# A hybrid diffusion step in fp32: input modulation split differently over the engines, and a spread-out residual chain

## Chip, cores and metric

One core of one Trainium2 chip. The metric is the device time of one execution in microseconds (us); the profile is one execution on the same core, with the time of every instruction.

## What is computed

The reference is one inference step of a two-layer backbone on 640 tokens (128 context tokens and 512 latent ones) of width 2048, in fp32. Cut to what matters here:

```python
for l in range(DEPTH):
    hp = rmsnorm(xp, norm_pre[l]) * (1.0 + sc_p[:, None]) + sh_p[:, None]
    hs = rmsnorm(xs, norm_pre[l]) * (1.0 + sc_s[:, None]) + sh_s[:, None]
    ...
    xp = xp + g_p[:, None] * rmsnorm(op, norm_post[l])
    xs = xs + g_s[:, None] * rmsnorm(os_, norm_post[l])
```

Between the two stands the layer's mixer: an input projection of h, attention (layer 0) or retention (layer 1), a gate, and an output projection to op and os_. Shift sh and scale sc are vectors over the 2048 features, one for the context and one for the latent tokens; they come from a small product of the conditioning with w_ada.

## The kernel before

Everything lies transposed: features on the 128 partitions in 16 tiles (KT = 16), the 640 tokens along the free dimension. Tokens come in two groups, columns 0 to 384 (GROUPS[0], 128 context and 256 latent tokens) and 384 to 640 (GROUPS[1]). An fp32 product is made of three faster ones: each operand is split into a rounded high half and the remainder (hi and lo for activations, whi and wlo for weights), and hi x whi, lo x whi and hi x wlo are summed in PSUM. A split takes a copy with rounding on ScalarE (ACT) and a subtraction on VectorE (DVE).

**Slots.** The four big projections are one list of slots. A slot has one piece of weight of 128 x 512: its load on the SP queue, its split (split_slot, lines 277 and 278, four slots ahead: there are four buffers for whi and wlo), and its products on TensorE (PE, line 1374; line 1315 for a layout that is transposed). A 128-column block of output takes four slots. In an output projection the 16 blocks of group 0 come first and then those of group 1, 64 slots each.

**Lanes.** All other work is queued by hand in lanes (class Lane). An item of a lane is a list of stages. One call of step() runs one stage of each item in flight, oldest first, and then takes up to `new` further items whose needs are done, and runs their first stage. step_all() is called once per slot ahead of the slot's products; the split of the slot four ahead is issued behind them. Thus the program order of every engine is fixed by the lanes, and an instruction that waits holds all that is behind it on its engine.

**The start (lines 286 to 479).** For 64 steps u, a piece of w_ada (512 KB of "ada" rows, on the SP queue, eight buffers) is multiplied with the conditioning on TensorE (a_mm, line 328). Four steps give one row of shift and scale for one tile kt: row() adds four partial rows on VectorE (lines 370 and 372), turn() transposes them on TensorE (line 376), mods() forms sh and am on VectorE. The input x lies in y. Before the loop its squares are summed and the norm factor is spread over all partitions (rbc). The lanes of the start run in the order d_l, s_l, x_l, w_l, h_l. In s_l, scale_x multiplies a tile of x by rbc on POOL (GpSimd). In x_l, mod_x applies am and sh on VectorE (two instructions, since context and latent tokens have different columns), and split_x makes hi on ScalarE and lo on VectorE. w_l splits the first weights (lines 415 and 416). d_l multiplies (first_dense, line 425): each step's products stand on TensorE between the a_mm of two steps.

**The residual chain (queue_chain, from line 911).** When the last block of a group's output projection is evacuated, its chain is queued. For layer 0 it holds: the norm (n1 with sums on TensorE, n2, rbc); for each tile n a residual item res(n), with r1 multiplying y by rbc (on VectorE for even n, on POOL for odd n), r2 adding x on VectorE, r3 squaring on ScalarE, r4 adding to the sum acc2 on POOL, and a store to x1; then a second norm; then for each tile an item hk(n): h1 multiplies by rbc on VectorE, h2 applies am and sh on POOL, h3 makes hi on ScalarE, h4 makes lo on VectorE. The last h4 sets ("h1", group). The chain of group 0 so runs beside the 64 slots of group 1's output projection, with one item begun per slot (new = 1); the chain of group 1 runs beside the first 32 slots of the next projection w_in_odd, which are for group 0 alone, with two per slot (new = 2). Before w_in_odd uses a group, all steps that are left up to ("h1", group) are run at once. Beside the chain evac_out squares every finished block on ScalarE and adds it on POOL (line 886), once in four slots.

Of the kernel before, what the change touches and what calls it, by code (L numbers as in the profile page):

```python
# [11 lines left out]
F32 = mybir.dt.float32  # L12
F32R = mybir.dt.float32r
BF16 = mybir.dt.bfloat16
AF = mybir.ActivationFunctionType
ALU = mybir.AluOpType
# [6 lines left out]
T = TP + TS  # L23
# [139 lines left out]
def body(tc, io):  # L163
    nc = tc.nc
# [6 lines left out]
    hi = main.tile([128, KT, T], F32R, name="hi")  # L171
    lo = main.tile([128, KT, T], F32R, name="lo")
    y = main.tile([128, KT, T], F32, name="y")
# [8 lines left out]
    sh = [main.tile([128, KT, 2], F32, name=f"sh{l}") for l in range(2)]  # L182
    am = [main.tile([128, KT, 2], F32, name=f"am{l}") for l in range(2)]
# [47 lines left out]
    def parts(c0, c1):  # L231

        return [(a, b, v) for a, b, v in ((c0, min(c1, TP), 0), (max(c0, TP), c1, 1)) if a < b]

    def unperm(dst, m0, nm):

        return dst.rearrange("p (r m c) -> p m r c", r=8, m=4)[:, m0:m0 + nm]
# [18 lines left out]
    for job, (w, kind, role, col, gs) in enumerate(STREAM):  # L256
        u0 = FIRST_UNIT[BLOCK_AT[w, kind, col]]
        n = UNITS[kind]
# [23 lines left out]
    with ExitStack() as st:  # L282
        s1 = st.enter_context(tc.tile_pool(name="s1", bufs=1))
        sraw = st.enter_context(tc.tile_pool(name="sraw", bufs=SRAW))
        x = y
# [47 lines left out]
        done = set()  # L333
        h_l, d_l = Lane(done), Lane(done)
# [14 lines left out]
        rbc = s1.tile([128, T], F32, name="rbc0")  # L349
# [15 lines left out]
        def queue_h(kt):  # L365
            t = {}

            def row():
                t["row"] = r = s1.tile([2, 256], F32, name="adarow", bufs=2)
                nc.vector.tensor_copy(r, rowps[kt][0:2, :256])  # L370
                for j in range(1, 4):
                    nc.vector.tensor_tensor(r, r, rowps[kt][32 * j:32 * j + 2, :256], op=ALU.add)

            def turn():
                for i in range(2):
                    nc.tensor.transpose(rowps[kt][:, 256 + 2 * i:258 + 2 * i], t["row"][:, 128 * i:128 * i + 128],
                                        ident[:2, :2])

            def mods():
                ps = rowps.pop(kt)  # L380
                nc.vector.tensor_scalar(sh[0][:, kt, :], ps[:, 256:258], cols[:, 0, 2, kt:kt + 1], None, op0=ALU.add)
                nc.vector.tensor_scalar(am[0][:, kt, :], ps[:, 258:260], bsc1[:, kt:kt + 1], cols[:, 0, 0, kt:kt + 1],
                                        op0=ALU.add, op1=ALU.mult)
                done.add(("mods", kt))

            def scale_x():
                nc.gpsimd.tensor_tensor(x[:, kt, :], x[:, kt, :], rbc, op=ALU.mult)
                done.add(("scaled", kt))

            def mod_x():  # L390
                u = x[:, kt, :]
                for a, b, v in parts(0, T):
                    nc.vector.tensor_scalar(u[:, a:b], u[:, a:b], am[0][:, kt, v:v + 1], sh[0][:, kt, v:v + 1],
                                            op0=ALU.mult, op1=ALU.add)

            def split_x():
                u = x[:, kt, :]
                nc.scalar.activation(hi[:, kt, :], u, AF.Copy)
                nc.vector.tensor_tensor(lo[:, kt, :], u, hi[:, kt, :].bitcast(F32), op=ALU.subtract)
                done.add(("h", kt))  # L400

            h_l.add([row, None, turn, mods], [("row", kt)])
            s_l.add([scale_x], ["rbc"] + ([("mods", kt - 1)] if kt > 1 else []))
            x_l.add([mod_x, split_x], [("mods", kt), ("scaled", kt)])

        def queue_d(q):
            ns, kt, after = FIRST_SEQ[q]
# [30 lines left out]
            w_l.add([split_w], ["rbc", ("w", q), ("row", min(after, KT - 1))] + ([("d", q - 3)] if q > 2 else []))  # L438
            d_l.add([None] + [first_dense(n) for n in range(4)], [("h", kt), ("wsplit", q)])

        x_l, s_l, w_l = Lane(done), Lane(done), Lane(done)
        for kt in range(KT):
            queue_h(kt)
        for q in range(len(FIRST_SEQ)):
            queue_d(q)
        lanes0 = (d_l, s_l, x_l, w_l, h_l)

        def squares(i):
            for kt in range(4 * i, 4 * i + 4):
# [39 lines left out]
    done = set()  # L489
    heads = Lane(done)  # L490
    rope = Lane(done)
    chain = Lane(done)
# [418 lines left out]
    def queue_chain(l, gi):  # L911
# [50 lines left out]
        def res(n):  # L962
            v = y[:, n, a:b]
            t = {}

            def r1():
                (nc.gpsimd if n % 2 else nc.vector).tensor_tensor(v, v, st["rbc"][:, :w], op=ALU.mult)  # L967

            def r2():
                nc.vector.tensor_tensor(v, v, c["x", 8 * gi + n // 2][:, n % 2, :w], op=ALU.add)  # L970

            def store():
                if n % 2:
                    nc.sync.dma_start(dst[:, n - 1:n + 1, a:b], y[:, n - 1:n + 1, a:b])
                    i = 8 * gi + n // 2
                    if i < 3:
                        free("kkq"[i])
                    else:
                        load_x(l, i + 3)

            def r3():
                t["sq"] = cp.tile([128, 384], F32, name="sq2", bufs=2)
                nc.scalar.activation(t["sq"][:, :w], v, AF.Square)

            def r4():
                if n == 0:
                    c["acc2", gi] = cp.tile([128, w], F32, name=f"acc2{gi}")
                    nc.vector.tensor_copy(c["acc2", gi], t["sq"][:, :w])
                elif n == KT - 1:
                    c["acc2", gi] = [c["acc2", gi], t["sq"]]  # L990
                    done.add(("acc2", l, gi))
                else:
                    nc.gpsimd.tensor_tensor(c["acc2", gi], c["acc2", gi], t["sq"][:, :w], op=ALU.add)

            return [r1, r2, r3, r4, store]

        def hk(n):
            t = {}

            def h1():  # L1000
                t["u"] = cp.tile([128, 384], F32, name="u", bufs=6)
                nc.vector.tensor_tensor(
                    t["u"][:, :w], y[:, n, a:b], st["rbc"][:, :w], op=ALU.mult)

            def h2():
                u = t["u"]
                for a2, b2, v in parts(a, b):
                    nc.gpsimd.tensor_scalar(u[:, a2 - a:b2 - a], u[:, a2 - a:b2 - a], am[1][:, n, v:v + 1],  # L1008
                                            sh[1][:, n, v:v + 1], op0=ALU.mult, op1=ALU.add)

            def h3():
                nc.scalar.activation(hi[:, n, a:b], t["u"][:, :w], AF.Copy)

            def h4():
                nc.vector.tensor_tensor(lo[:, n, a:b], t["u"][:, :w], hi[:, n, a:b].bitcast(F32), op=ALU.subtract)
                if n == KT - 1:
                    done.add(("h1", gi))

            return [h1, h2, h3, h4]

        chain.add([None, n1("acc"), None, n2, flag("rbc")])
        for n in range(0, KT, 2 if last else 1):
            chain.add((res_pair if last else res)(n), [("rbc", l, gi)] if n == 0 else ())
            if last and gi == 0:
                chain.add([None])
        if not last:
            chain.add([None, None, None, n1("acc2"), None, n2, flag("rbc2")], [("acc2", l, gi)])
            for n in range(KT):
                chain.add(hk(n), [("rbc2", l, gi)] if n == 0 else ())


    R = {}
# [484 lines left out]
```

## Time and profile before

| what | value |
| --- | --- |
| median of 3 runs | 2555.88 us (2555.37 to 2557.2) |
| the profiled execution | 2555.74 us |
| its span in the profile | 2553.9 us |
| TensorE busy | 2466.1 us (97%) |
| VectorE busy | 1507.5 us (59%) |
| ScalarE busy | 994.0 us (39%) |
| POOL busy | 485.3 us (19%) |
| moved by DMA | 347.12 MB, 136 GB/s on average |

The span runs from the first to the last instruction. A busy TensorE is not TensorE at its peak: products are pipelined, their ends are modelled, and two may overlap in the table. So the pace of a stage is read from the distance of the starts of something that returns in every fourth slot, and not from the busy share. An arrow with a name behind a time says what the engine had stood idle for.

### The profile page before, as it was taken

The page shows a single profiled execution, that of the slowest core. Times are in us where ns is not written, and L with a number is a line of the kernel's source. Part 1 is how long each engine was busy: PE and PEld are TensorE (multiplying, and loading weights), DVE is VectorE, ACT ScalarE, POOL GpSimd, SP SyncE. Part 2 cuts the span into 40 slices and gives each one's busy share as a digit, 9 for nine tenths or more (in the row PEclk, how much of TensorE's full clock was granted, in tenths as well). Part 3 has the DMA queues.
Part 4 walks back from the last instruction along what each step waited for, and adds up shares of the span by engine and source line. Part 5 has one row for each costly group of instructions (what it writes and reads, how often), then busy time and mean ns, then how long its engine had stood idle before and what let it go on. Part 6 is the DMA issues. An engine that isn't in the chain of part 4 may idle for free.

```text
span 2553.9 us, 45697 instructions
## 1 busy us (share of the span) xinstructions
PE 2466.1 (97%) x17808; PEld 2386.2 (93%) x17808; DVE 1507.5 (59%) x2770; ACT 994.0 (39%) x2108; POOL 485.3 (19%) x525
## 2 busy tenths in 40 slices
PE   4999999999999999998999999999999999999997
PEld 2689898999999999997999999999999999999996
DVE  7568788887777775348663445252525355364364
ACT  2233454543343435444543333232323333254443
POOL 5012221112112110117430101010101011011132
PEclk9999999999999999999999999999999999999998
DMA  9856444445545532445554221212121221215373
GB/s 347 321 173 185 146 141 135 135 134 186 175 153 174 177 126 88 161 134 189 172 162 140 70 80 62 88 59 87 59 89 62 83 73 61 87 56 176 124 236 131
DMA packets 186442, 347.12 MB, mean 136 GB/s; under 512 B 20912, under 2 KB 45872, under 8 KB 185712
## 3 DMA queue, kind: packets, MB, share of 16 engines
q1 hardware_dynamic: 182368, 333.25, 39.7%
q0 software_dynamic: 3712, 10.82, 1.2%
q8 instruction: 139, 2.28, 0.4%
q14 instruction: 79, 0.65, 0.1%
q10 hardware_dynamic: 144, 0.13, 0.0%
HBM read 325.51 MB, written 15.99 MB: 134 GB/s over the span
## 4 chain that ended last, share of the span: by engine, by line
PE 67%; DVE 4%; issue 2%; POOL 2%; DMA 1%; ACT 1%; SPq 0%; DVEq 0%; ACTq 0%; POOLq 0%
PE ps_d L1374 47%; PE ps_d L1315 12%; PE ps_O L1254 2%; POOL u L1008 1%; DVE wlo L278 1%; DVE adaacc L800 1%; PE ps_O L1158 1%; PE ps_S L1158 1%; DMA wraw<-i_wpack 1%; DVE y L970 1%; PE ps_O L749 1%; PE ps_T L1232 1%; PE ps_S L1246 1%; ACT whi L277 0%; DVE y L967 0%
## 5 line engine op out<-in xcount | busy, mean ns | idle before, releaser
L1374 PE MATMUL ps_d<-hi,whi 128*128 128x384 f32 (+1 forms) x3808 | 1000.8, 316 | 3.4 <-ACT whi L277 3.2
L1374 PE MATMUL ps_d<-hi,wlo 128*128 128x384 f32 (+1 forms) x3808 | 977.9, 311 | 15.8 <-DVE wlo L278 15.5
L1374 PE MATMUL ps_d<-lo,whi 128*128 128x384 f32 (+1 forms) x3808 | 973.5, 309 | 0.0
L278 DVE TENSOR_TENSOR wlo<-wraw,whi 128x512 fp32r<-128x512 f32 x732 | 570.8, 783 | 609.0 <-ACT whi L277 601.7
L1374 PEld LDWEIGHTS ps_d<-hi,wlo 128*128 128x128 f32 x3808 | 629.7, 189 | 22.3 <-DVE wlo L278 21.9
L1374 PEld LDWEIGHTS ps_d<-hi,whi 128*128 128x128 f32 x3808 | 634.3, 189 | 15.3 <-ACT whi L277 4.3
L1374 PEld LDWEIGHTS ps_d<-lo,whi 128*128 128x128 f32 x3808 | 629.3, 189 | 0.0
L277 ACT ACTIVATE whi<-wraw 128x512 fp32r<-128x512 f32 x732 | 455.7, 626 | 439.7 <-PE ps_d L1374 222.0
L800 DVE SCALAR_TENSOR_TENSOR adaacc<-adaraw,cvec,adaacc 128x512 f32<-128x512 f32 x400 | 278.0, 746 | 5.8 <-POOL adaacc L798 5.7
L798 POOL TENSOR_TENSOR adaacc<-adaacc,adaraw 128x512 f32<-128x512 f32 x80 | 102.9, 1286 | 687.6 <-ACT adaraw L797 687.6
L1315 PE MATMUL ps_d<-whi,hi 128*128 128x256 f32 x960 | 151.0, 287 | 0.7 <-ACT qT L650 0.7
L1315 PE MATMUL ps_d<-whi,lo 128*128 128x256 f32 x960 | 144.4, 280 | 0.0
L1315 PE MATMUL ps_d<-wlo,hi 128*128 128x256 f32 x960 | 144.4, 280 | 0.0
L797 ACT ACTIVATE adaraw<-adaraw,cvec 128x512 f32<-128x512 f32 x80 | 57.9, 724 | 207.7 <-DVE adaacc L800 144.6
L1315 PEld LDWEIGHTS ps_d<-whi,hi 128*128 128x128 f32 x960 | 128.1, 189 | 4.9 <-issue 1.4
L886 POOL TENSOR_TENSOR acc<-acc,sq 128x384 f32<-128x384 f32 (+1 forms) x56 | 56.1, 1002 | 397.7 <-ACT sq L882 397.4
L1315 PEld LDWEIGHTS ps_d<-whi,lo 128*128 128x128 f32 x960 | 126.6, 188 | 0.0
L1315 PEld LDWEIGHTS ps_d<-wlo,hi 128*128 128x128 f32 x960 | 126.5, 188 | 0.0
L694 ACT ACTIVATE p<-p,small 128x384 f32<-128x384 f32 (+1 forms) x64 | 42.9, 671 | 149.8 <-DVE small L686 149.8
L1150 DVE SCALAR_TENSOR_TENSOR fr<-ps_T,kdec,fr 128x256 fp32r<-128x256 f32 x64 | 31.0, 484 | 95.7 <-ACT fr L1149 95.7
L1266 POOL TENSOR_TENSOR mv<-mv,mhalf 128x1 f32<-128x1 f32 x40 | 22.0, 550 | 299.6 <-DVE mv L1265 289.2
L1218 POOL TENSOR_TENSOR qS<-q,qS 128x256 fp32r<-128x256 f32 x32 | 25.2, 789 | 278.8 <-ACT qS L1217 278.8
(251 smaller groups left out, 2502.2 us busy)
## 6 DMA issues: line engine op xcount, KB each, us to landing
wraw<-i_wpack SPq DMA_DIRECT2D x732, 256.0 KB, 2.8
adaraw<-i_ada SPq DMA_DIRECT2D x256, 256.0 KB, 2.7
sraw<-i_ada SPq DMA_DIRECT2D x64, 512.0 KB, 5.7
y<-i_xTp SPq DMA_DIRECT2D x4, 1280.0 KB, 8.6
wf<-i_wfirst SPq DMA_DIRECT2D x20, 256.0 KB, 5.5
bias<-i_biasB POOLq DMA_DIRECT2D x8, 640.0 KB, 4.7
x_scratch<-y SPq DMA_DIRECT2D x8, 384.0 KB, 3.9
xres<-x_scratch SPq DMA_DIRECT2D x8, 384.0 KB, 6.4
```

Of the source, the lines that this page charges most:

```text
L277: nc.scalar.activation(h, r, AF.Copy)
L278: nc.vector.tensor_tensor(l, r, h.bitcast(F32), op=ALU.subtract)
L694: nc.scalar.activation(p[:, :nk], src, AF.Exp, bias=sm[:, 0:1], accum_out=sm[:, 1:2])
L797: nc.scalar.activation(r, r, AF.Copy, scale=cvec[:, kt, 1:2])
L798: nc.gpsimd.tensor_tensor(accs[1], accs[1], r, op=ALU.add)
L800: nc.vector.scalar_tensor_tensor(accs[v], r, cvec[:, kt, v:v + 1], accs[v], op0=ALU.mult, op1=ALU.add)
L886: nc.gpsimd.tensor_tensor(c["acc", gi], c["acc", gi], sq[:, :w], op=ALU.add)
L1150: nc.vector.scalar_tensor_tensor(t[:, 1, :], ps[:, :256], R["kdec"][:, d, h:h + 1], t[:, 0, :].bitcast(F32), op0=ALU.mult, op1=ALU.subtract)
L1158: mm(ps[:, 256 * d:256 * d + 256], lhsT=k[:, kp, 128 * d:128 * d + 128], rhs=v[:, vp, ch, :], start=(i == 0), stop=(i == 2))
L1254: mm(ab, lhsT=t["q"][:, qp, d, :], rhs=t["S"][d][sp].rearrange("p i e -> p (i e)"), start=(d == 0 and i == 0), stop=(d == 1 and i == 2))
L1315: mm(pss[j][:, o:o + 256], lhsT=xp[:, k, c0:c0 + 128], rhs=wp[:, 256 * kk:256 * kk + 256], start=(i == 0 and kk == 0 and p == 0 and t in ( ...
L1374: mm(pss[gi][:, :b - a], lhsT=wp[:, 128 * kk:128 * kk + 128], rhs=xp[:, k, a:b], start=(k == 4 * i0 and p == 0), stop=(k == KT - 1 and p = ...
```

## The change

The modulation is taken apart in three steps, for both layers. mod_scale makes x times rbc times am in one VectorE instruction per part (context and latent tokens: two instructions where the columns hold both). mod_split then adds the shift twice: on ScalarE, as the bias of the copy that rounds to hi, and on VectorE, in the subtraction that gives lo. The lane s_l with its multiplication on POOL is dropped, and x_l waits for rbc itself. In the residual chain r1 is on VectorE for every n. The four stages of hk become two. For the first group, an empty item stands behind every second residual item and every second hk item.

```diff
--- before.py
+++ after.py
@@ -232,6 +232,20 @@
 
         return [(a, b, v) for a, b, v in ((c0, min(c1, TP), 0), (max(c0, TP), c1, 1)) if a < b]
 
+    def mod_scale(u, src, rb, l, n, a, b):
+
+        for a2, b2, v in parts(a, b):
+            nc.vector.scalar_tensor_tensor(u[:, a2 - a:b2 - a], src[:, a2 - a:b2 - a], am[l][:, n, v:v + 1],
+                                           rb[:, a2 - a:b2 - a], op0=ALU.mult, op1=ALU.mult)
+
+    def mod_split(u, l, n, a, b):
+
+        for a2, b2, v in parts(a, b):
+            nc.scalar.activation(hi[:, n, a2:b2], u[:, a2 - a:b2 - a], AF.Identity, bias=sh[l][:, n, v:v + 1])
+        for a2, b2, v in parts(a, b):
+            nc.vector.scalar_tensor_tensor(lo[:, n, a2:b2], u[:, a2 - a:b2 - a], sh[l][:, n, v:v + 1],
+                                           hi[:, n, a2:b2].bitcast(F32), op0=ALU.add, op1=ALU.subtract)
+
     def unperm(dst, m0, nm):
 
         return dst.rearrange("p (r m c) -> p m r c", r=8, m=4)[:, m0:m0 + nm]
@@ -383,25 +397,15 @@
                                         op0=ALU.add, op1=ALU.mult)
                 done.add(("mods", kt))
 
-            def scale_x():
-                nc.gpsimd.tensor_tensor(x[:, kt, :], x[:, kt, :], rbc, op=ALU.mult)
-                done.add(("scaled", kt))
-
             def mod_x():
-                u = x[:, kt, :]
-                for a, b, v in parts(0, T):
-                    nc.vector.tensor_scalar(u[:, a:b], u[:, a:b], am[0][:, kt, v:v + 1], sh[0][:, kt, v:v + 1],
-                                            op0=ALU.mult, op1=ALU.add)
+                mod_scale(x[:, kt, :], x[:, kt, :], rbc, 0, kt, 0, T)
 
             def split_x():
-                u = x[:, kt, :]
-                nc.scalar.activation(hi[:, kt, :], u, AF.Copy)
-                nc.vector.tensor_tensor(lo[:, kt, :], u, hi[:, kt, :].bitcast(F32), op=ALU.subtract)
+                mod_split(x[:, kt, :], 0, kt, 0, T)
                 done.add(("h", kt))
 
             h_l.add([row, None, turn, mods], [("row", kt)])
-            s_l.add([scale_x], ["rbc"] + ([("mods", kt - 1)] if kt > 1 else []))
-            x_l.add([mod_x, split_x], [("mods", kt), ("scaled", kt)])
+            x_l.add([mod_x, split_x], [("mods", kt), "rbc"])
 
         def queue_d(q):
             ns, kt, after = FIRST_SEQ[q]
@@ -438,12 +442,12 @@
             w_l.add([split_w], ["rbc", ("w", q), ("row", min(after, KT - 1))] + ([("d", q - 3)] if q > 2 else []))
             d_l.add([None] + [first_dense(n) for n in range(4)], [("h", kt), ("wsplit", q)])
 
-        x_l, s_l, w_l = Lane(done), Lane(done), Lane(done)
+        x_l, w_l = Lane(done), Lane(done)
         for kt in range(KT):
             queue_h(kt)
         for q in range(len(FIRST_SEQ)):
             queue_d(q)
-        lanes0 = (d_l, s_l, x_l, w_l, h_l)
+        lanes0 = (d_l, x_l, w_l, h_l)
 
         def squares(i):
             for kt in range(4 * i, 4 * i + 4):
@@ -964,7 +968,7 @@
             t = {}
 
             def r1():
-                (nc.gpsimd if n % 2 else nc.vector).tensor_tensor(v, v, st["rbc"][:, :w], op=ALU.mult)
+                nc.vector.tensor_tensor(v, v, st["rbc"][:, :w], op=ALU.mult)
 
             def r2():
                 nc.vector.tensor_tensor(v, v, c["x", 8 * gi + n // 2][:, n % 2, :w], op=ALU.add)
@@ -999,34 +1003,26 @@
 
             def h1():
                 t["u"] = cp.tile([128, 384], F32, name="u", bufs=6)
-                nc.vector.tensor_tensor(
-                    t["u"][:, :w], y[:, n, a:b], st["rbc"][:, :w], op=ALU.mult)
+                mod_scale(t["u"], y[:, n, a:b], st["rbc"], 1, n, a, b)
 
             def h2():
-                u = t["u"]
-                for a2, b2, v in parts(a, b):
-                    nc.gpsimd.tensor_scalar(u[:, a2 - a:b2 - a], u[:, a2 - a:b2 - a], am[1][:, n, v:v + 1],
-                                            sh[1][:, n, v:v + 1], op0=ALU.mult, op1=ALU.add)
-
-            def h3():
-                nc.scalar.activation(hi[:, n, a:b], t["u"][:, :w], AF.Copy)
-
-            def h4():
-                nc.vector.tensor_tensor(lo[:, n, a:b], t["u"][:, :w], hi[:, n, a:b].bitcast(F32), op=ALU.subtract)
+                mod_split(t["u"], 1, n, a, b)
                 if n == KT - 1:
                     done.add(("h1", gi))
 
-            return [h1, h2, h3, h4]
+            return [h1, h2]
 
         chain.add([None, n1("acc"), None, n2, flag("rbc")])
         for n in range(0, KT, 2 if last else 1):
             chain.add((res_pair if last else res)(n), [("rbc", l, gi)] if n == 0 else ())
-            if last and gi == 0:
+            if gi == 0 and (last or n % 2):
                 chain.add([None])
         if not last:
             chain.add([None, None, None, n1("acc2"), None, n2, flag("rbc2")], [("acc2", l, gi)])
             for n in range(KT):
                 chain.add(hk(n), [("rbc2", l, gi)] if n == 0 else ())
+                if gi == 0 and n % 2:
+                    chain.add([None])
 
 
     R = {}
```

## Rows read from the trace of the kernel before

**Rows 1.** The page, section 1: busy us (share of the span) and instructions, TensorE.
```profile
PE 2466.1 (97%) x17808; PEld 2386.2 (93%) x17808; DVE 1507.5 (59%) x2770; ACT 994.0 (39%) x2108; POOL 485.3 (19%) x525
```

**Rows 2.** Busy time by stretch: length; PE, PEld, DVE, ACT, POOL; PEclk, DMA share, GB/s.
```profile
30.00:40.00 10.00, 4.79 (x62) 1.81 (x60) 7.90 (x11) 3.06 (x6) 8.95 (x6) 0.80 0.96 363
...
60.00:70.00 10.00, 10.00 (x87) 6.20 (x86) 7.25 (x17) 3.29 (x9) 0.32 (x1) 1.00 0.92 316
```

**Rows 3.** Order of time at the start, TensorE: start, us, instruction, idle before it.
```profile
34.88 0.28 PE L376 MATMUL ps_S<-ident,adarow 2*128 2x2 f32 x2 [3.08 <-DVE adarow L372]
...
41.51 0.37 PE L376 MATMUL ps_T<-ident,adarow 2*128 2x2 f32 x2 [3.65 <-DVE adarow L372]
...
58.21 0.28 PE L376 MATMUL ps_T<-ident,adarow 2*128 2x2 f32 x2 [1.19 <-DVE adarow L372]
```

**Rows 4.** Order of time at the start, VectorE.
```profile
31.52 1.62 DVE L416 TENSOR_TENSOR wlo<-wf,whi 128x512 fp32r<-128x512 f32 x1 [2.65 <-ACT whi L415]
...
35.71 2.12 DVE L393 TENSOR_SCALAR y<-y,am,sh 128x128 f32<-128x128 f32 x2
37.75 2.03 DVE L416 TENSOR_TENSOR wlo<-wf,whi 128x512 fp32r<-128x512 f32 x1
...
60.78 0.68 DVE L416 TENSOR_TENSOR wlo<-wf,whi 128x512 fp32r<-128x512 f32 x1
...
65.77 0.80 DVE L393 TENSOR_SCALAR y<-y,am,sh 128x128 f32<-128x128 f32 x2
```

**Rows 5.** TensorE from 1126 us (order of time), then the chain: start, us, what.
```profile
1130.24 0.28 PE L1374 MATMUL ps_d<-hi,whi 128*128 128x256 f32 x1
...
1253.74 0.79 PE ps_T L209 x8
...
1259.32 10.61 PE ps_d L1374 x60
```

**Rows 6.** Order of time, POOL, second half of the output projection: L886 alone.
```profile
1165.03 1.17 POOL L886 TENSOR_TENSOR acc<-acc,sq 128x256 f32<-128x256 f32 x1
...
1175.66 1.18 POOL L886 TENSOR_TENSOR acc<-acc,sq 128x256 f32<-128x256 f32 x1
...
1215.83 1.03 POOL L886 TENSOR_TENSOR acc<-acc,sq 128x256 f32<-128x256 f32 x1
...
1225.15 1.04 POOL L886 TENSOR_TENSOR acc<-acc,sq 128x256 f32<-128x256 f32 x1
...
1240.72 0.74 POOL L886 TENSOR_TENSOR acc<-acc,sq 128x256 f32<-128x256 f32 x1 [5.08 <-ACT sq L882]
1246.48 0.74 POOL L886 TENSOR_TENSOR acc<-acc,sq 128x256 f32<-128x256 f32 x1 [5.02 <-ACT sq L882]
```

**Rows 7.** Order of time, VectorE, residual stage.
```profile
1140.59 0.69 DVE L278 TENSOR_TENSOR wlo<-wraw,whi 128x512 fp32r<-128x512 f32 x1
1141.19 0.55 DVE L970 TENSOR_TENSOR y<-y,k 128x384 f32<-128x384 f32 x1
1141.66 0.69 DVE L278 TENSOR_TENSOR wlo<-wraw,whi 128x512 fp32r<-128x512 f32 x1
...
1162.84 1.36 DVE L967 TENSOR_TENSOR y<-y,rbc 128x384 f32<-128x384 f32 x1
```

**Rows 8.** Groups of VectorE instructions: xcount, busy us, mean ns, idle before.
```profile
L800 DVE SCALAR_TENSOR_TENSOR adaacc<-adaraw,cvec,adaacc 128x512 f32<-128x512 f32 x400 | 278.0, 746 | 5.8 <-POOL adaacc L798 5.7
...
L1150 DVE SCALAR_TENSOR_TENSOR fr<-ps_T,kdec,fr 128x256 fp32r<-128x256 f32 x64 | 31.0, 484 | 95.7 <-ACT fr L1149 95.7
```

**Rows 9.** Groups of ScalarE instructions from 65 to 155 us.
```profile
L398 ACT ACTIVATE hi<-y 128x640 fp32r<-128x640 f32 x12 | 8.9, 739 | 45.5 <-DVE y L393 45.5
```

**Rows 10.** Order of time, POOL, before the residual's sums begin.
```profile
1137.33 1.98 POOL L967 TENSOR_TENSOR y<-y,rbc 128x384 f32<-128x384 f32 x2 [2.84 <-ACT rbc L228]
```

**Rows 11.** Waits of TensorE, 1231 to 1321 us: us in total, times, longest.
```profile
PE ps_d L1374 <- DVE wlo L278: 1.5, 2, 0.9
```

**Rows 12.** Waits of the SP queue, 0 to 60 us: us in total, times, longest.
```profile
SPq L308 <- PE ps_S L328: 17.8, 8, 7.8
```

## The prediction

> **What bounds the kernel now.** The page comes first: TensorE is busy for 97% of the span [rows 1], so only stretches in which its queue runs dry can be won. Next the busy time by stage. In the first 60 us TensorE has gaps, from 60 us on it has none, and the DMA share is high all along [rows 2]. Third, TensorE's order of time at the start: it stands three times before L376, the transposes of the modulation row, for 3.08, 3.65 and 1.19 us, each time for VectorE's additions of L372 [rows 3]. VectorE is late there because POOL multiplies x by the norm at the same time (L387): the same low-half subtraction takes 1.62 us at 31.5 us and 0.68 us once POOL is quiet, the next one 2.03, and the pair of modulations 2.12 against 0.80 [rows 4].
>
> The other dry stretch is the second half of the layer-0 output projection, where the first token group's residual chain runs beside 64 slots for the second group. Its first product starts at 1130.24. The norm sums of the second group's chain start at 1253.74, behind one slot of the next projection, and such a slot takes 10.61 / 5 = 2.12 us [rows 5]. So the 64 slots took 1253.74 - 2.12 - 1130.24 = 121.4 us. One POOL addition of L886 falls in every fourth slot, which makes it a clock of the pace [rows 6]: 5.76 us per four undisturbed slots, or 1.44 each; 10.63, or 2.66, while the residual is made; 9.32, or 2.33, while h is made. Undisturbed, 64 slots take 92.2 us, and the two norms' small products between them add some 3.7 (estimated from the starts between which they stand in this order of time), 95.9 together. So 25.5 us are lost. Of what the slow paces add, 16 x 1.22 + 16 x 0.89 = 19.5 + 14.2 = 33.7, the split weights made ahead hide (33.7 - 25.5) / 2 = 4.1 per stage.
>
> Who sets the paces? In the residual stage VectorE: alone, an addition of 384 columns takes 0.55 us and the next starts after 0.47, a subtraction of 512 starts 0.60 ahead of the next, but with POOL adding beside it the 384 take 1.36, 0.81 more [rows 7]. Per slot VectorE has 0.60 for the weight, 0.47 for r2 and half of 0.47 for r1, 1.305. POOL has r4, half an r1 and a quarter of L886 (256 columns, two thirds as long): 1.667 units of 384. 1.305 + 1.667 x 0.81 = 2.66, just the pace measured. In the h stage POOL's L1008 sets it; the two parts keep POOL full.
>
> **The change, part by part.** *Start, x input.* POOL's 16 multiplications leave, and their wait; each step now issues two VectorE instructions with scalar (128 and 512 columns), two ScalarE ones and two VectorE ones, where two, one and one stood beside POOL's. Such an instruction takes 0.746 us for 512 and 0.484 for 256 columns [rows 8], so about 0.35 for 128: a pair about 1.0. That is 0.2 more than the modulation pair alone, and 0.2 more than the subtraction it replaces (640 columns at the rate of the 512 in [rows 4], about 0.8). ScalarE's rounding took 0.739 us in one [rows 9]; in two with a bias no row shows it, between 0.74 and 1.48. I take 0.95, as only a second fixed part is added. From 60 us on VectorE and ScalarE have room for all of this under TensorE, with no cost; if that cover went, 16 x 0.2 us would show. Along the path: the weight half ends 0.95 us earlier, so the first transpose starts at 33.9. Modulation (1.0 for 2.12) and the second weight half (0.6 for about 1.95) bring the second transpose from 41.51 to about 38.1, 3.4 us earlier. The first dense products then follow the low half, 0.2 longer than before, some 3.5 us earlier. The third row's stall of 1.19 goes too, as a step of TensorE is longer than VectorE's work without POOL. Together **4.7 us**. Late next is TensorE itself. The bounds: 0, if the ada rows do not land earlier (below), and 6.6, if the TensorE clock, granted at 0.80 in this stage [rows 2], stays up.
>
> *Residual, group 1 (384 columns).* Eight r1 move from POOL to VectorE; a free slot after every second step makes 16 steps last 24 slots. Counted in the lane: first r1 in slot 5, last in 28 less one, 27; the sum complete in 30; first h in 36, last in 58, its halves in 59 of 64. The next projection, which wants all of it, still opens without a burst. Per three slots VectorE has 3 x 0.60 + 4 x 0.47 = 3.68, TensorE 4.32. But L993's sums and L886 stay on POOL, 2 + 0.75 x 0.67 = 2.5 units: + 2.03, 5.7, or 1.90 per slot. So VectorE still sets the pace, 24 x 0.46 = 11.0 late, less 4.1 hidden: a loss of 6.9 in place of 19.5 - 4.1 = 15.4. **Gain 8.5.** The bounds: no loss (15.4), if the sums fall where VectorE pauses, and the last rival's loss below.
>
> One bound between is POOL's own length. Alone, a POOL operation of 384 columns lasts 1.98 / 2 = 0.99 us [rows 10]; if VectorE stood still all that time, 0.99 would be added and not 0.81. The new pace would be (3.68 + 2 x 0.99 + 0.75 x 0.74) / 3 = 2.07 and the loss 4.1 us larger. But the old pace would then have been 1.305 + 1.5 x 0.99 + 0.25 x 0.74 = 2.98, and 2.66 was measured, so I take 0.81. The Trainium skill's page "SBUF — State Buffer", section "SBUF: two separate sides", states this stronger form: a VectorE operation with two SBUF inputs and a reading GpSimd operation exclude each other for the whole instruction. By that rule the sum below would be 2535.5; the trace does not agree with the full length.
>
> *h, group 1.* L1008 leaves POOL (two instructions per step). VectorE gets two pairs (128 and 256) for two whole operations. With the overlap of 0.08 a pair is 0.27 + 0.40 = 0.67. Per three slots 1.80 + 4 x 0.67 + 0.41 for L886 = 4.9, 1.63 per slot: 24 x 0.19 = 4.6 late, 4.1 hidden, a loss of 0.5 in place of 14.2 - 4.1 = 10.1. **Gain 9.6.** Lower half and rounding now stand in one step, so VectorE waits for ScalarE, with the next h and the next weight half queued behind it; ScalarE's work per slot (some 1.2 us, estimated by the rate of [rows 9]) is under 1.44, so the lead carries it. Bounds: 2.6, if each pair takes a third more (5.8 per three slots), and 10.1.
>
> *Group 2 (256 columns)* has no free slots, but its r1 and modulation leave POOL too. TensorE lost 1.5 us there [rows 11]; I take it as won. Bounds 0 and 1.5. The stores and residual loads on SP keep their order and number and are only spread out, so they cost nothing while the weight loads run several slots ahead; without that lead a load would wait for a store's r2.
>
> **Sum.** 4.7 + 8.5 + 9.6 + 1.5 = 24.3 us from the profiled execution's 2555.74 (span 2553.9, 1.84 around it; the median of the runs is 2555.88): **2531.4 us**. TensorE works without a pause from 60 us to the end of that stage (its first slice is in [rows 2]) and is 97% busy over the span [rows 1], so the stages behind are bound by it and a gain is not given back.
>
> **Rivals.** *The start waits for DMA instead.* DMA is 0.92 to 0.96 busy in these slices [rows 2]; the rows wanted earlier might not be there. Against it: in the first 60 us SP stood 17.8 us until products into one of the two PSUM banks had freed a buffer [rows 12], so the loads were held by TensorE. It would give 2555.74 - 19.6 = 2536.1.
>
> *POOL's whole length.* If 0.99 is added as worked out above, 2531.4 + 4.1 = 2535.5. Against it: the old pace.
>
> *The residual keeps its old pace.* If 2.66 per slot held for 24 slots, because VectorE's added products meet POOL as the old ones did, the loss would be 24 x 1.22 - 4.1 = 25.2, 9.8 more than before: 2555.74 - 4.7 - 9.6 - 1.5 + 9.8 = 2549.7. For it: the fit of 0.81 is one stage's. Against it: POOL's work per slot halves.
>
> *Slower.* If nearly every VectorE operation of the residual met one of POOL's, a slot would cost (3 x 1.41 + 4 x 1.28) / 3 = 3.12 us, as 0.81 is added to each. A loss of 24 x 1.68 - 4.1 = 36.2 in place of 15.4 gives 2555.74 + 20.8 - 15.8 = 2560.7. It decides from 1.44 + (15.4 + 15.8 + 4.1) / 24 = 2.91 per slot on. Against it: POOL has 2.75 operations to meet VectorE's 7 in three slots.
>
> **How the numbers follow.** Forecast 0.70, DMA start 0.09, whole length 0.08, old pace 0.07, slower 0.06. 0.2% is 5.1 us, about what a measurement of this kernel tells from no change. The old pace lies just beyond it, so I give 0.04 of its 0.07 to faster and 0.03 to the same: faster 0.91, same 0.03, slower 0.06. Low end: no residual loss (6.9 less) and some more at the start, 2522. High end: the DMA start with the larger loss of the residual by POOL's whole length, 2536.1 + 4.1 = 2540. This holds the first three cases except their tails, some 0.8.
>
> **What would show it.** After the change L346 and L213 alone remain on POOL before 60 us; the second transpose starts near 38 us; the dense products of the first stage end some 5 us earlier. L886 comes every 7.6 us in the residual and every 5.8 to 6.5 in the h stage; the second half of the output projection takes about 103 us. A wait of TensorE for ada rows before 60 us, or L886 every 10 us, shows a rival. If the 64 slots take as long as before, the prediction is wrong at its core.

## The result, and the profile after

The changed kernel takes **2534.12 us** (median of four runs, 2533.36 to 2534.7), against 2555.62 for the kernel before in the same comparison: a ratio of 0.9913, 95% interval 0.9898 to 0.9929. The profiled execution took 2534.7 us with a span of 2532.9, 21.0 less than before. Forecast were 2531.4 and a range from 2522 to 2540. The result lies in the range, 2.7 us above the forecast: the h stage gained 2.3 us less than its term and the second group 0.9 less, while the start gained 1.0 more.

Page, section 1, of the changed kernel, which answers to [rows 1]:
```profile
PE 2459.2 (97%) x17808; PEld 2383.1 (94%) x17808; DVE 1499.3 (59%) x2834; ACT 1006.8 (40%) x2140; POOL 389.6 (15%) x445
```
POOL lost 95.7 us of work in 80 instructions. VectorE has 64 instructions more and is 8.2 us less busy: it no longer stands so long against POOL. How much of that TensorE got, the stages show.

**The start.** Busy time by stretch, changed kernel, columns as in [rows 2]:
```profile
30.00:40.00 10.00, 5.99 (x77) 3.25 (x77) 7.00 (x18) 3.44 (x7) 0.00 (x0) 1.00 0.98 352
40.00:50.00 10.00, 10.00 (x89) 6.22 (x87) 8.13 (x20) 3.29 (x6) 0.00 (x0) 1.00 1.03 408
50.00:60.00 10.00, 10.00 (x89) 6.20 (x88) 6.62 (x17) 1.65 (x3) 0.00 (x0) 1.00 1.03 408
```
TensorE works without a pause from 40 us on, POOL does nothing, and the granted clock stays at 1.00. The transposes of the modulation row in order of time, TensorE, then VectorE's instructions of the first step (answers to [rows 3, 4]):
```profile
34.77 0.28 PE L390 MATMUL ps_S<-ident,adarow 2*128 2x2 f32 x2 [2.02 <-DVE adarow L386]
...
38.88 0.28 PE L390 MATMUL ps_T<-ident,adarow 2*128 2x2 f32 x2 [1.99 <-DVE adarow L386]
...
52.29 0.28 PE L390 MATMUL ps_T<-ident,adarow 2*128 2x2 f32 x2
```
```profile
32.35 0.69 DVE L420 TENSOR_TENSOR wlo<-wf,whi 128x512 fp32r<-128x512 f32 x1 [3.46 <-ACT whi L419]
...
35.54 1.01 DVE L238 SCALAR_TENSOR_TENSOR y<-y,am,rbc 128x128 f32<-128x128 f32 x2
36.47 0.69 DVE L420 TENSOR_TENSOR wlo<-wf,whi 128x512 fp32r<-128x512 f32 x1
...
38.76 0.99 DVE L246 SCALAR_TENSOR_TENSOR lo<-y,sh,hi 128x128 fp32r<-128x128 f32 x2
```
The weight half takes 0.69 us for 1.62, the modulation pair 1.01 for 2.12, the two stalls are 2 us for 3.08 and 3.65, and the third is gone.

**The output projection's second half.** First products of three norm sums and the broadcast of the second norm, TensorE, changed kernel:
```profile
1126.00 0.28 PE L209 MATMUL ps_T<-ones,acc 128*128 128x1 f32 x2
...
1179.84 0.28 PE L209 MATMUL ps_T<-ones,acc 128*128 128x1 f32 x2
...
1184.88 0.91 PE L227 MATMUL ps_S<-rdiag,ones 128*128 128x128 f32 x6 [0.66 <-DVE rdiag L219]
...
1232.68 0.28 PE L209 MATMUL ps_T<-ones,acc 128*128 128x1 f32 x2
```
Of these sums the first lies in the second slot and the third a slot of the next projection behind the 64. Between them the kernel before took 121.90 us (1131.68 to 1253.58), the changed one 106.68. By the forecast's undisturbed 95.9 us for 64 slots the same stretch would be 95.9 - 1.44 + 2.12 = 96.6; so the loss fell from 25.3 to 10.1 us. The 64 slots themselves took 1232.68 - 2.12 - 1124.56 = 106.0 us, where 103 were forecast. POOL's adds of the second group's squares, one per four slots, are the clock as in [rows 6]; first those of the residual stage, then of the h stage:
```profile
1145.81 1.19 POOL L890 TENSOR_TENSOR acc<-acc,sq 128x256 f32<-128x256 f32 x1
...
1168.89 1.18 POOL L890 TENSOR_TENSOR acc<-acc,sq 128x256 f32<-128x256 f32 x1
1176.77 1.18 POOL L890 TENSOR_TENSOR acc<-acc,sq 128x256 f32<-128x256 f32 x1 [1.99 <-ACT sq L886]
...
1195.54 0.90 POOL L890 TENSOR_TENSOR acc<-acc,sq 128x256 f32<-128x256 f32 x1 [5.52 <-ACT sq L886]
...
1207.91 0.98 POOL L890 TENSOR_TENSOR acc<-acc,sq 128x256 f32<-128x256 f32 x1 [4.62 <-ACT sq L886]
...
1227.20 0.98 POOL L890 TENSOR_TENSOR acc<-acc,sq 128x256 f32<-128x256 f32 x1 [4.60 <-ACT sq L886]
```
There are 16 slots from 1145.81 to 1176.77 and 20 from 1195.54 to 1227.20: 30.96 / 16 = 1.94 us a slot and 31.66 / 20 = 1.58. But two items take three slots and the addition comes every fourth, so the distances repeat only after twelve slots. Over twelve they give 23.08 / 12 = **1.92** us a slot (1145.81 to 1168.89; forecast 1.90) and 19.29 / 12 = **1.61** (1207.91 to 1227.20; forecast 1.63).

### The profile page after: what moved, and what is told of

It is laid out like the page before. It is cut to its first block, busy times and chain, and to the rows that moved or that the text cites. A ratio compares the mean times of both kernels' runs of the same rounds, so it can differ in the third digit from the quotient of the medians.

```text
span 2532.9 us, 45640 instructions
## 1 busy us (share of the span) xinstructions
PE 2459.2 (97%) x17808; PEld 2383.1 (94%) x17808; DVE 1499.3 (59%) x2834; ACT 1006.8 (40%) x2140; POOL 389.6 (15%) x445
## 4 chain that ended last, share of the span: by engine, by line
PE 69%; DVE 4%; issue 2%; ACT 1%; DMA 1%; POOL 0%; SPq 0%; DVEq 0%; ACTq 0%; POOLq 0%
PE ps_d L1370 49%; PE ps_d L1311 12%; PE ps_O L1250 2%; DVE wlo L292 1%; DVE adaacc L804 1%; PE ps_O L1154 1%; PE ps_S L1154 1%; PE ps_O L753 1%; PE ps_T L1228 1%; ACT whi L291 1%; PE ps_S L1242 1%; DMA wraw<-i_wpack 0%; PE ps_T L742 0%; DVE y L974 0%; PE ps_T L1141 0%
## 5 line engine op out<-in xcount | busy, mean ns | idle before, releaser
L1235 ACT ACTIVATE sS<-sT 128x128 fp32r<-128x128 f32 x40 | 12.4, 311 | 147.9 <-DVE sT L1234 147.9
```

## The experiments

All take the changed kernel as their base. A table holds what the text uses of the traces: when the first norm sum starts, and the time from there to the second, third and fourth one. The total moves with the start by some 2 us; the stretches between the sums repeat to 0.03 us where nothing in them was changed, and are the finer measure.

| kernel | median us | first sum | to second | to third | to fourth |
|---|---|---|---|---|---|
| before | 2555.62 | 1131.68 | 50.23 | 71.67 | 37.26 |
| changed | 2534.12 | 1126.00 | 53.84 | 52.84 | 36.68 |
| start only | 2551.2 | 1126.65 | 50.23 | 71.67 | 37.27 |
| no free slots | 2544.33 | 1125.45 | 49.53 | 67.04 | 36.66 |
| r1 on POOL | 2538.58 | 1126.50 | 57.30 | 53.43 | 36.69 |
| h on POOL | 2542.05 | 1127.65 | 53.85 | 60.09 | 36.68 |
| POOL out of ring | 2537.37 | 1126.53 | 53.85 | 55.25 | 36.66 |
| longer gap | 2535.04 | 1127.10 | 58.15 | 48.05 | 36.68 |
| sums on VectorE | 2528.67 | 1125.77 | 49.23 | 52.55 | 35.26 |
| sums and gap | 2528.56 | 1125.76 | 53.54 | 48.25 | 35.26 |
| stores on POOL's queue | 2531.96 | 1126.15 | 49.79 | 53.44 | 35.25 |
| all sums on VectorE | 2530.08 | 1127.59 | 48.17 | 53.37 | 35.25 |

Where free slots are missing the second sum lies eight slots earlier, where the gap is longer three slots later; there the second and third stretch are read together.

**Start only**: the new x input with the old chain.
```
-                nc.vector.tensor_tensor(v, v, st["rbc"][:, :w], op=ALU.mult)
+                (nc.gpsimd if n % 2 else nc.vector).tensor_tensor(v, v, st["rbc"][:, :w], op=ALU.mult)
...
-            return [h1, h2]
+            return [h1, h2, h3, h4]
...
-            if gi == 0 and (last or n % 2):
+            if last and gi == 0:
```


> The x input in three steps; the residual chain as before. Theory (the start and the chain are two separate stages and their gains add): the first product of the second half of the output projection starts 5.7 us earlier than in the kernel before, as in the changed kernel, that half takes 121.4 us as before, and the time is some 5.5 us under the kernel before, about 2550. Rival (the earlier start is lost again at the DMA-heavy hand-over): within 2 us of the kernel before.

Measured: 2551.2 us, ratio 0.998 (0.997 to 0.9989). The first sum comes 5.03 us earlier, and the three stretches behind it are those of the kernel before to 0.01 us: the start's gain passes through the kernel and touches nothing else.

**No free slots**: the chain's instructions as changed, the empty items taken out.
```
-            if gi == 0 and (last or n % 2):
+            if gi == 0 and last:
...
-                if gi == 0 and n % 2:
-                    chain.add([None])
```


> The changed kernel without the empty items of the first group. Theory (VectorE's rate is its own lengths and 0.81 us per POOL operation of 384 columns; the free slots bring that rate near TensorE's): 0.60 + 0.94 + 1.167 x 0.81 = 2.49 us per slot in the residual stage and 0.60 + 1.34 + 0.13 = 2.07 in the h stage, so losses of 16 x 1.05 - 4.1 = 12.6 and 16 x 0.63 - 4.1 = 6.1 us in place of 6.9 and 0.5: some 11 us over the changed kernel, about 2545. Rival (POOL's leaving does it, and the free slots only shift the same work): within 2 us of the changed kernel, 2534.

Measured: 2544.33 us, ratio 0.9953 (0.9938 to 0.9968). POOL's clock in the residual stage:
```profile
1158.78 1.17 POOL L890 TENSOR_TENSOR acc<-acc,sq 128x256 f32<-128x256 f32 x1 [1.38 <-ACT sq L886]
1168.74 1.18 POOL L890 TENSOR_TENSOR acc<-acc,sq 128x256 f32<-128x256 f32 x1 [1.38 <-ACT sq L886]
```
9.96 / 4 = 2.49 us a slot (10.76 in the round before, in which POOL still worked off an addition that had been kept out for 4.74 us). In the forecast's terms a slot without free ones has 0.60 + 2 x 0.47 of VectorE and 1 + 0.25 x 0.67 additions of POOL at 0.81, 2.49 together. So 0.81 holds at a second load; and of the chain's 15.2 us, 9.9 (116.57 - 106.68) come only with the free slots.

**r1 on POOL**: the eight odd products of the first group go back, with the free slots kept.
```
-                nc.vector.tensor_tensor(v, v, st["rbc"][:, :w], op=ALU.mult)
+                (nc.gpsimd if n % 2 and gi == 0 else nc.vector).tensor_tensor(v, v, st["rbc"][:, :w], op=ALU.mult)
```


> The changed kernel with the first group's odd r1 back on POOL, free slots kept. Theory: per three slots 3 x 0.60 + 3 x 0.47 + 3.5 x 0.81 = 6.05 us, 2.02 per slot for 1.90, so 24 x 0.12 = 2.8 us over the changed kernel, about 2537. Rival (keeping POOL off the products is the gain): half or more of the stage's gain goes, 4 us or more over the changed kernel.

Measured: 2538.58 us, ratio 0.9932 (0.9917 to 0.9946); 4.5 us over the changed kernel, 4.05 of it between the first and the third sum. POOL's clock reads 32.69 / 16 = 2.04 us a slot from 1147.49 to 1180.18, where the sum with 0.81 gives 2.02. The pace agrees with the theory; the time is over the 2.8 us that I made of it and on the rival's side: the residual stage got 3.46 us longer, where 24 x (2.04 - 1.92) = 2.9 are due by the pace, and the h stage 0.59, as less lead came over.

**h on POOL**: h back in its four old steps (VectorE's product, POOL's modulation, ScalarE's high half, VectorE's low half), residual products and free slots as changed.
```
-                mod_scale(t["u"], y[:, n, a:b], st["rbc"], 1, n, a, b)
+                nc.vector.tensor_tensor(
+                    t["u"][:, :w], y[:, n, a:b], st["rbc"][:, :w], op=ALU.mult)
...
-            return [h1, h2]
+            return [h1, h2, h3, h4]
```


> The changed kernel with the four-step h of the kernel before (modulation on POOL), free slots kept. Theory: POOL needs 2 x 2.08 + 0.75 x 1.03 = 4.93 us per three slots, 1.64 per slot against 1.58 measured for the changed kernel, so the free slots alone give nearly the whole gain of this stage: 0 to 3 us over the changed kernel, 2534 to 2537. Rival (POOL's leaving is the gain of the h stage): 6 us or more over the changed kernel, 2540 or more.

Measured: 2542.05 us, ratio 0.9944 (0.993 to 0.9959). My theory fell: the h stage is 7.25 us longer. Its waits from 1181 to 1242 us (us in total, times, longest):
```profile
ACT hi L1016 <- POOL u L1012: 21.9, 11, 2.9
DVE wlo L292 <- ACT whi L291: 18.5, 16, 2.4
POOL u L1012 <- DVE u L1006: 10.1, 8, 1.9
```
POOL waits for VectorE for 10.1 us, so it is not full. ScalarE stands 21.9 us in front of POOL with the next weight's high half queued behind, VectorE waits 18.5 us for that high half, and its next h1 stands behind: a ring of three queues, each taken in order. The new theory was tried next.

**POOL out of the ring**: an empty step, in the first group, between POOL's and ScalarE's.
```
-            return [h1, h2, h3, h4]
+            return [h1, h2] + [None] * (gi == 0) + [h3, h4]
```


> The kernel with the first group's h modulation back on POOL in four steps, which took 2542.05 us, with one empty step between POOL's step and ScalarE's, in the first group alone, so that ScalarE's rounding no longer stands in its queue waiting for POOL, with the weight split behind it. Theory (the 8 us of that kernel come from a ring of waits taken in order: VectorE, POOL, ScalarE, and the next weight split behind it): the pace of the h stage falls from 1.93 us a slot to VectorE's own work with POOL's cost on it, (3 x 0.60 + 4 x 0.47 + 2 x 0.81) / 3 = 1.77 us, or to 1.58 if POOL costs VectorE less there, so 2534 to 2538 us. Rival (POOL's work on VectorE's operands, not the order of the waits, makes the 8 us): pace near 1.93, 2541 to 2543 us.

Measured: 2537.37 us, ratio 0.9924 (0.9912 to 0.9937). One empty step takes 4.84 of the 7.25 us back. POOL's clock reads 41.93 / 24 = 1.75 us a slot (1188.94 to 1230.87), against 46.42 / 24 = 1.93 without the step (1190.23 to 1236.65) and the 1.77 expected. So two thirds of what POOL's modulation costs here is the order of the waits. The third that is left goes with the pace that was expected from POOL's price on VectorE; no run took it apart further. The Trainium skill's page "PSUM — Partial Sum Buffer", section "Engine vs sequencer instructions", calls the queues of ScalarE, VectorE and GpSimd strict FIFO; the trace agrees, since ScalarE's wait on POOL kept back a high half that didn't need POOL.

**Sums on VectorE**: the adds of the second norm's squares leave POOL, in both groups.
```
-                    nc.gpsimd.tensor_tensor(c["acc2", gi], c["acc2", gi], t["sq"][:, :w], op=ALU.add)
+                    nc.vector.tensor_tensor(c["acc2", gi], c["acc2", gi], t["sq"][:, :w], op=ALU.add)
```


> The changed kernel with one operation moved: the adds of the second norm's squares (r4) go from POOL to VectorE, in both groups. Theory (each POOL add of 384 columns costs VectorE 0.81 us, more than the 0.47 us that the add costs on VectorE itself): a residual round of three slots goes from 5.9 us to about 3 x 0.60 + 6 x 0.47 + 0.5 x 0.81 = 5.0 us, 1.68 us a slot where the changed kernel shows 1.94; the stage's loss falls from 7.2 to about 2 us, about 2529 us in all. Rival (what counts is how much VectorE has to do, and 14 adds more are 6.6 us): 1.94 us a slot or more, 2535 to 2541 us.

Measured: 2528.67 us (2528.24 to 2529.61), ratio 0.989 (0.9877 to 0.9904): **faster than both kernels**, and where the theory put it. VectorE does 28 additions more and the stretches shrink by 4.61, 0.29 and 1.42 us. The last is group 2, without free slots: POOL's sums were what had kept its loss. The intervals of the two ratios overlap by 0.0006, but the slowest run here is 3.7 us under the fastest of the changed kernel, and the stretches alone give 6.3 us.

**Longer gap**: the h stage starts three slots later.
```
-            chain.add([None, None, None, n1("acc2"), None, n2, flag("rbc2")], [("acc2", l, gi)])
+            chain.add([None] * (6 if gi == 0 else 3) + [n1("acc2"), None, n2, flag("rbc2")], [("acc2", l, gi)])
```


> The changed kernel with three empty items more between the first group's last residual item and its second norm, so that the h stage starts three slots later. Theory (the h stage's loss of 3.0 us, where 0.5 was forecast, comes from a lead of the split over TensorE that had been used up in the residual stage and was not rebuilt in the six slots between): three more undisturbed slots give back 3 x (1.56 - 1.44) = 0.4 us of lead and let the late weight loads catch up, and the h stage loses 1 to 2 us less: 2532 to 2533 us. Rival (the h stage loses by its own pace of 1.58 us a slot whatever the lead): no change from the changed kernel, 2534 us, or, if the later h delays the next group, over 2535 us.

Measured: 2535.04 us, ratio 0.9914 (0.99 to 0.9927): no change in all, the rival's number. The trace shows a little of the theory. From the chain of waits, the longest undisturbed piece behind the second norm, first of the changed kernel, then of this one:
```profile
1185.78 15.85 PE ps_d L1370 x132
```
```profile
1191.14 30.15 PE ps_d L1370 x251
```
TensorE runs 21 slots before VectorE catches it, not 11, so there is more lead; but from the first sum to the third it is worth 106.68 - 106.20 = 0.48 us, not 1 to 2. TensorE's weight loads wait for low halves behind the second norm for 1.0 us where they waited for 1.4.

**Sums and gap**: the diffs of the two kernels above, together.

> Both edits, the adds of squares on VectorE and three empty items more ahead of the second norm. If each theory holds alone and the lead is what joins the two stages, the gap gives less here, since the residual stage uses up less lead: about 2528 us, within 1 us of the kernel with the adds moved alone. If the gap is worth the same 1 to 2 us in both, about 2527 us. If the adds on VectorE cost their own length, 2535 us or more, like that kernel alone.

Measured: 2528.56 us, ratio 0.989 (0.9875 to 0.9905). First to third sum: 101.79 us, with the gap unchanged 101.78. Where the residual stage uses up less lead, the gap is worth nothing: in these two traces the late low halves cost 1.0 us for 1.4, but TensorE's wait at the second norm grew from 0.3 to 0.8.

**Stores on POOL's queue**, with the sums on VectorE. Shortly before the second norm the chain of waits passes through a weight load that takes over 5 us from its issue, first in the changed kernel, then with the sums on VectorE:
```profile
1175.36 5.42 DMA wraw<-i_wpack
```
```profile
1170.05 5.57 DMA wraw<-i_wpack
```
The edit, beside that of the sums:
```
-                    nc.sync.dma_start(dst[:, n - 1:n + 1, a:b], y[:, n - 1:n + 1, a:b])
+                    nc.gpsimd.dma_start(dst[:, n - 1:n + 1, a:b], y[:, n - 1:n + 1, a:b])
...
-                        load_x(l, i + 3)
+                        load_x(l, i + 3, nc.gpsimd)
```


> The kernel with the adds of squares on VectorE (2528.67 us), in which the layer-0 chain's stores and the residual loads that follow them are issued by POOL's queue and not by SP's. Theory (TensorE's 0.8 us at the second norm come from a weight load that lands late, since it was issued behind a store and a residual load on SP): the load that reaches ScalarE near 1175.6 us comes over 1 us earlier, the norm's column is ready before TensorE wants it, and the h stage loses 0.8 us less; 2527.5 to 2528 us. Rival (the load is late because VectorE frees the weight buffers late and in bunches, so that the queue's order is nothing): 2528 to 2529.5 us with the same waits of TensorE at the second norm, 0.3 us or more.

Measured: 2531.96 us, ratio 0.9905 (0.9889 to 0.9922): slower than without the move, and my theory fell. ScalarE's wait for weight loads went from 3.8 to 1.0 us between 1125 and 1235 us, yet TensorE's wait at the second norm grew from 0.3 to 1.22:
```profile
1181.55 0.91 PE L227 MATMUL ps_S<-rdiag,ones 128*128 128x128 f32 x6 [1.22 <-DVE rdiag L219]
```
The stores are off SP, but the late load is still there, and later. The chain of waits of this kernel, ahead of that broadcast:
```profile
1170.29 0.69 DVE wlo L292
...
1170.99 6.45 DMA wraw<-i_wpack
...
1179.37 0.69 DVE wlo L292
1180.06 0.08 DVE msq L212
```
The load is issued as soon as VectorE's low half has freed its buffer, as the rival has it, so the queue's order was not what made it late; the rival's 2528 to 2529.5 us was missed too. Whether the norm would be earlier without a late load, this run can't tell. The chain says what stands before the norm: its first step on VectorE (msq) lies in order behind low halves that wait for high halves, and those for the load. Why the load takes 6.45 us here is open. Of the 3.4 us by which the profiled executions differ, 0.4 lie before the first sum, 1.4 between the first and the fourth, and 1.5 behind.

**All sums on VectorE**: the sums of the second group's own squares too.
```
-                    nc.gpsimd.tensor_tensor(c["acc", gi], c["acc", gi], sq[:, :w], op=ALU.add)
+                    nc.vector.tensor_tensor(c["acc", gi], c["acc", gi], sq[:, :w], op=ALU.add)
```


> The kernel with the adds of squares on VectorE (2528.67 us), in which the last POOL operation beside these two stages goes too: the adds of the second group's own squares, one per weight slot of the second group, on VectorE. Theory of the price alone: such an add of 256 columns costs VectorE 0.54 us on POOL (two thirds of 0.81) and about 0.32 by itself, so a residual round of three slots gets 0.75 x 0.22 = 0.17 us shorter, 24 slots 1.3 us, and the h stage as much: 2527 to 2528 us. Rival (order): the add waits for ScalarE's square, which waits for TensorE to finish the slot, and it stands in VectorE's queue ahead of weight splits that run slots ahead of TensorE; the lead is cut at every such add, and the time goes up, to 2531 us or more.

Measured: 2530.08 us, ratio 0.9897 (0.988 to 0.9913); the interval overlaps that of the sums on VectorE. Between the first and the third sum 101.54 us, 0.24 less than there; the profiled executions differ by 1.9 us, as their first sums do (1.8). Neither theory had the size: the residual stage gains 1.06, the h stage loses 0.82, with a wait of 1.69 us for the second norm's diagonal. The gain by price and the loss by order nearly cancel.

## Why the prediction was right, and where 2.7 us went

**The start: right, 5.7 for 4.7.** The first transpose came at 34.77, not 33.9: the broadcast of the norm (L227) took TensorE 2.43 us here, 1.48 before, and the weight half stood until 32.35. ScalarE's two roundings took 2 x 0.563 = 1.13 us (mean of 22, from 65 to 155 us) where 0.95 was taken, hidden as forecast. The second came at 38.88, against 38.1. What more than made up for it is the clock. In the kernel before TensorE had stood 3.08 and 3.65 us and was busy 4.49 of 8 us, at the lower level (0.50, 1.2 GHz); after, the same stretch shows 1.00. Before, then after:
```profile
38.00:46.00 8.00, 4.49 (x25) 2.43 (x26) 7.76 (x11) 1.69 (x3) 8.00 (x5) 0.50 1.03 407
```
```profile
38.00:46.00 8.00, 7.12 (x64) 4.47 (x68) 6.34 (x16) 1.65 (x3) 0.00 (x0) 1.00 1.03 409
```
The eleven profiles with the new start bear it out: where the clock stays at 1.00 from 30 to 50 us (changed, no free slots, sums on VectorE, sums and gap, stores on POOL's queue) the first sum starts at 1125.45 to 1126.15; with 0.83 in the first of these slices at 1126.50 to 1126.65; with 0.83 to 0.86 in the second at 1127.10 to 1127.65. So with the same code the start is worth 4.0 to 6.2 us, all inside the forecast's bounds of 0 and 6.6, and that the changed kernel's profile shows 1.0 more than forecast is the luck of its clock. DMA was no bound: it reads 1.03 from 40 to 60 us with TensorE never waiting, and SP still waits for PSUM-bound products, 17.6 us for 17.8 in [rows 12]. The DMA rival falls.

**Residual: right.** The loss is 53.84 - 46.5 = 7.3 us, forecast 6.9 (46.5 is 31 slots of 1.44 and half of the norms' 3.7). An instruction on 384 columns that runs free and one that meets POOL's addition still show the price, as in [rows 7]; POOL's addition first, then VectorE's two:
```profile
1142.30 1.19 POOL L997 TENSOR_TENSOR acc<-acc,sq 128x384 f32<-128x384 f32 x1 [1.78 <-ACT sq L987]
```
```profile
1141.46 0.54 DVE L971 TENSOR_TENSOR y<-y,rbc 128x384 f32<-128x384 f32 x1
...
1142.53 1.36 DVE L974 TENSOR_TENSOR y<-y,k 128x384 f32<-128x384 f32 x1
```
The rivals "POOL's whole length" (2.07 a slot) and "the old pace" (2.66) fall with 1.92, 2.49 and 2.04 in three kernels, all within 0.02 of the sum with 0.81; with 0.99 the three would be 2.07, 2.72 and 2.25. Slower falls too: each POOL operation met about one of VectorE's, not each of VectorE's one of POOL's.

**h: the term that was mis-sized.** The pace was right, and a pair of products takes 0.66 start to start in the chain (forecast 0.67). But the loss is 52.84 - 50.05 = 2.8 us (32 slots of 1.44, one of 2.12, the norm's 1.85), not 0.5. The step that failed is "4.6 late, 4.1 hidden": I spread the hidden 33.7 - 25.5 evenly and gave the full 4.1 to each stage, though the residual stage uses the lead up and only six slots lie between. At 1.61 a slot 24 slots are 4.1 late. From 1181 to 1235 us TensorE's products wait 0.66 for the second norm's diagonal and 0.3 for low halves, and its weight loads (PEld) 1.4 for low halves (us in total, times, longest):
```profile
PEld ps_d L1370 <- DVE wlo L292: 1.4, 4, 0.6
```
Without the norm's wait 2.1 of the 4.1 show, so only some 2 were hidden and not the full 4.1. That the lead is a part of it, the longer gap shows (21 undisturbed slots for 11), at 0.5 us; and with the residual stage's loss cut to 2.7, the h stage still loses 2.5. So the lead explains a part, and the wait at the second norm is another. The chain of waits of the changed kernel, from the high half behind the load of 1175.36 to the broadcast:
```profile
1180.89 0.59 ACT whi L291
...
1182.71 0.69 DVE wlo L292
1183.40 0.08 DVE msq L212
...
1184.88 0.91 PE ps_S L227 x6
```
The norm's first step on VectorE (msq) lies in order behind the low half of 1182.71. No run took the late load out of this chain, so how much of the loss is its doing stays open.

The forecast's bound for h's gain, "2.6, if each pair takes a third more", was not reached. The reason that I gave for POOL as h's limit, that "the two parts keep POOL full", was not the whole: with free slots POOL waits 10.1 us and the stage is still 7.25 us longer.

**Group 2: 0.6 for 1.5** (37.26 to 36.68). I took all of TensorE's loss there as won, but POOL's sums of r4 stayed; with them on VectorE the stretch falls to 35.26.

**Sum**: 5.68 + 15.22 + 0.58 = 21.48 us by the fourth sum, and the profiled execution is 21.0 shorter. Of the 0.5 between them 0.4 lies between the last two norm sums (97.05 us for 96.64), a stretch that takes 95.6 to 98.0 us in the eleven kernels that have the same code there (all but "all sums on VectorE"). So the gain was kept to the end, as forecast.

## What to carry to other kernels

Price work on POOL by what it adds to VectorE, not by what POOL has free: here 0.81 us per operation of 384 columns that gets in beside VectorE's, more than the 0.47 us that the same addition costs on VectorE. A lead that hides a slow stage is spent once: count it once over stages that follow closely. And before an operation is put on a third engine, look at which queue will stand waiting for it, and what is behind it there; one empty step in a pipeline can be worth more than the engine.

## What the runs showed of the hardware

POOL can be kept out for long. In the kernel with the sums on VectorE, POOL and VectorE in order of time:
```profile
1144.34 8.09 POOL L890 TENSOR_TENSOR acc<-acc,sq 128x256 f32<-128x256 f32 x1 [5.02 <-ACT sq L886]
```
```profile
1148.66 0.69 DVE L292 TENSOR_TENSOR wlo<-wraw,whi 128x512 fp32r<-128x512 f32 x1
1149.27 0.56 DVE L997 TENSOR_TENSOR acc<-acc,sq 128x384 f32<-128x384 f32 x1
1149.74 0.56 DVE L974 TENSOR_TENSOR y<-y,xres 128x384 f32<-128x384 f32 x1
...
1152.10 0.88 DVE L292 TENSOR_TENSOR wlo<-wraw,whi 128x512 fp32r<-128x512 f32 x1 [0.27 <-ACT whi L291]
```
An addition that takes 0.74 us elsewhere takes 8.09, while VectorE runs two-input instructions without a gap at their own lengths; POOL gets through when VectorE pauses for 0.27 us. The same addition took 8.08 us in "sums and gap" and 8.07 in "stores on POOL's queue". The Trainium skill's page "SBUF — State Buffer", section "SBUF: two separate sides", has the pair's shared port as a lock that goes to whichever starts first, with the other blocked. The trace agrees in that POOL is blocked whole; that it stays blocked from one VectorE instruction to the next, for 7 us, is beyond what the page states. A VectorE instruction that meets POOL's loses 0.81 us where POOL's own length is 0.99 [rows 10], a little under what a block for the whole instruction would cost.
